# Hybrid decoder layer on one core: one 512-column product for the high and low parts of the tokens in the channel-major projections

## Chip, cores and metric

The kernel runs on one core of a Trainium2 chip. The metric is the device time of one execution in microseconds (us), as the median of several runs. TensorE multiplies matrices, VectorE (DVE) and ScalarE (ACT) do the elementwise work, GpSimd (POOL) a little of it, and SyncE (SP) issues the loads and stores.

## What is computed

One mixer layer on 256 tokens of width 2048, in float32. The input is normalised and modulated (h), a wide projection gives the inputs of two branches, gated DeltaNet (32 value heads of 128) and mLSTM (8 heads), and their merged output goes through one more projection and a norm. Cut to what matters here:

```python
h = rms_norm(x, norm_pre_w) * (1.0 + scale) + shift          # (256, 2048)
proj = h @ w_in                                              # all inputs of both branches
qkv = causal_conv_silu(gdn_qkv, gdn_conv_w)                  # 8192 channels
o_a = gated_delta_rule(q_a, k_a, v_a, g_log, beta)
y_a = (rms_norm(o_a, gdn_norm_w) * silu(gdn_z)) @ w_proj_gdn
qk = causal_conv_silu(ml_qk, mlstm_conv_w)                   # 2048 channels
h_b = mlstm_chunkwise(q_b, k_b, v_b, ml_i + b_i, ml_f + b_f)
y_b = (sigmoid(ml_o) * rms_norm(h_b) * silu(ml_z)) @ w_proj_mlstm
out = (sigmoid(gate_a) * y_a + sigmoid(gate_b) * y_b) @ w_out
x = x + gate * rms_norm(out, norm_post_w)

def causal_conv_silu(x, w):                                  # 4 taps along the tokens
    xp = pad(x, 3 rows in front)
    return silu(sum(xp[:, j:j + s] * w[j] for j in range(4)))
```

## The kernel before

**Two parts of each number.** Every projection is computed from float32 values split into a high part (rounded to fp32r by a copy on ScalarE, line 168) and a low part (value less high part, on VectorE or GpSimd, line 169). A product of two such numbers is three matmuls, `mm3` (lines 215 to 217): high x high, high x low, low x high, summed in PSUM. The tokens stand in `h_hi` and `h_lo`, two tiles of 16 chunks k of 128 rows by 256 tokens.

**The stream.** `Stream` (lines 62 to 113) runs through units of weights. A unit is one load of 1 MB (128 partitions by 2048 floats, issued by SP into one of three `raw` buffers) and two items of 1024 columns. For each item `prep_w` makes the high part `whi` and the low part `wlo` (four buffers each), some items ahead of TensorE; `use` then issues the matmuls; after that `Side.step` lets each side generator go on to its next `yield`. So one step of side work follows each item. The side generators hold the rest: convolution, attention, gates. `side.debt` (lines 37 to 55) is a rough count of VectorE time that the side work has asked for, with 2.1 us forgiven per step (`STEP_US`, line 26); only the triangular inverse (`base_inverse`) waits for it, through `side.room`.

**Stages.** A start part projects 14 groups while the modulation is still being computed. Then come eight periods of gated DeltaNet, `gdn_period`: a channel-major group of 512 channels (`add_proj_t`, pair 2zg), a token-major group for z (`add_proj_n`), and a second channel-major group (pair 2zg+1). Then four mLSTM pairs, each beginning with a channel-major group, the first also with the groups for o and z, the others with extra loads for the gate row. At the end are the two projections of the branches (`add_proj_y`) and the output projection. There are 20 channel-major groups in all.

**A channel-major group.** The weights are the stationary operand (128 channels) and the tokens the moving one (256 columns). Four units of four chunks k each; every item takes two chunks and all four channel blocks n, 24 matmuls. The four results share two PSUM banks of 512 columns (`pj` has four), and are complete only at the end of the group. `conv_silu` (lines 558 to 573) then scales them by the last tap on ScalarE (line 561), waits some steps, adds the other three taps on VectorE from PSUM (line 567), one channel block per step, and applies SiLU (line 570). `gdn_stage1` goes on with the products of q and k, the decay and the scaling; `base_inverse` inverts 32-row blocks on VectorE; `gdn_stage2` joins them with small matmuls and applies them one period later.

Of the kernel before, what the change touches and what calls it, by code (L numbers as in the profile page):

```python
# [7 lines left out]
F32 = mybir.dt.float32  # L8
# [7 lines left out]
P = 128  # L16
S = 256
# [99 lines left out]
def hybrid_layer_kernel(  # L117
# [41 lines left out]
    def load_w(src):  # L159
        raw = wp.tile([P, 2048], F32, name="raw", tag="raw", bufs=3)  # L160
        c = 0
        for s_ in src if isinstance(src, tuple) else (src,):
            SP.dma_start(raw[:, c:c + s_.shape[1]], s_)
            c += s_.shape[1]
        return raw
# [391 lines left out]

    def conv_silu(ps, taps, dst, hi=None, late=0):

        for n in range(4):  # L560
            A.activation(dst[:, n], ps[n // 2][:, (n % 2) * S:(n % 2 + 1) * S], AF.Copy, scale=taps(n, 3))
        yield from wait(1 + late)
        for n in range(4):
            src = ps[n // 2][:, (n % 2) * S:(n % 2 + 1) * S]
            side.debt += 1.45
            for sh in (1, 2, 3):
                V.scalar_tensor_tensor(dst[:, n, sh:], src[:, 0:S - sh], taps(n, 3 - sh), dst[:, n, sh:],  # L567
                                       op0=ALU.mult, op1=ALU.add)
            yield
        A.activation(dst, dst, AF.Silu)  # L570
        if hi is not None:
            A.copy(hi, dst[:, 0:2])
        yield

# [28 lines left out]

    def gdn_stage1(p, ps, res):

        z = p % 2
        qs = bp.tile([P, 4, S], F32, name="qs", tag="qs")
        qh = bp.tile([P, 2, S], F32R, name="qh", tag="qh", bufs=1)
        yield from conv_silu(ps, lambda n, j: late_c["gcv"][:, (p * 4 + n) * 4 + j:(p * 4 + n) * 4 + j + 1], qs, qh,
                             0 if z else 3)  # L610
        gb = decay_rows(2 * p)
# [25 lines left out]
        if z == 0:  # L637
            res["eq"] = bp.tile([P, 2, 2], F32, name="eq", tag="eq", bufs=3)
            res["rr"] = bp.tile([P, 2, 2, S], F32, name="rr", tag="rr")
        rk = bp.tile([P, 2], F32, name="rk", tag="rk")  # L640
# [84 lines left out]
    def gdn_stage2(zg, res, zr):  # L725
# [81 lines left out]
        for g, z, h, c in heads:  # L807
            T.matmul(po[z][:, h * P:(h + 1) * P], au[z][:, h, 0:128], ys[:, 0, c], start=True, stop=True)
            o2 = po[z][:, S + h * P:S + (h + 1) * P]
            T.matmul(o2, au[z][:, h, 128:256], ys[:, 0, c], start=True, stop=False)  # L810
            T.matmul(o2, au[z][:, h, 512:640], ys[:, 1, c], start=False, stop=True)  # L811
        so = bp.tile([P, 2, 2, 2], F32, name="so", tag="so")
        ons = []
# [39 lines left out]

    def period_tail(zg, ps, res, zr):
        yield from gdn_stage1(2 * zg + 1, ps, res)
        yield
        side.add(base_inverse(zg, res, zr), 2)

    zrs = [{} for _ in range(8)]

    def add_z(zg):
        def z_after(ps):
            sz = bp.tile([P, 2, 512], F32, name="sz", tag="sz", bufs=3)
            for b in range(2):
                A.activation(sz[:, b], ps[b], AF.Silu)
            zrs[zg]["sz"] = sz
        add_proj_n(16 + zg, z_after)

    def gdn_period(zg):
        res = {}  # L870
        add_proj_t(2 * zg, lambda ps: side.add(gdn_stage1(2 * zg, ps, res)))
        add_z(zg)
        add_proj_t(2 * zg + 1, lambda ps: side.add(period_tail(zg, ps, res, zrs[zg])))


    def mlstm_qk(m, ps, r):
        gb = decay_rows(32 + 2 * m)
        qk = bp.tile([P, 4, S], F32, name="mqk", tag="qs")
        yield from conv_silu(ps, lambda n, j: late_c["mcv"][:, (m * 4 + n) * 4 + j:(m * 4 + n) * 4 + j + 1], qk)
# [65 lines left out]
    def mlstm(m):  # L945
# [22 lines left out]
        def gate_after(ps, func):  # L968
            sg = bp.tile([P, 2, 512], F32, name="sg", tag="sz", bufs=3)
            for b in range(2):  # L970
# [13 lines left out]
        def gated():  # L984

            sg = bp.tile([P, 2, 512], F32, name="sg", tag="sz", bufs=3)
            SP.dma_start(sg, gate_dr[7 + m])
# [8 lines left out]
        gate_unit = add_gate_unit if m else None  # L996
        add_proj_t(24 + m, lambda ps: side.add(mlstm_qk(m, ps, r)), gate_unit)
        add_proj_n(28 + m, v_after, gate_unit)
# [55 lines left out]
    def add_proj_y(src_dr, w, nk2, mk, hf, after):  # L1054

        st_ = {}
        for k2 in range(nk2):
# [5 lines left out]
            def prep(h, raw, k2=k2):  # L1063
                if h == 0:
                    ahi = yp.tile([P, 2, S], F32R, name="yhi", tag="yhi", bufs=2)
                    alo = yp.tile([P, 2, S], F32R, name="ylo", tag="ylo", bufs=2)
                    split(st_[k2], ahi, alo)
                    st_["s", k2] = (ahi, alo)
                return prep_w(h, raw)
# [42 lines left out]
    def merge(hf, yb):  # L1112

        fp = late["fp"]
        if hf == 0:
            late["m"] = (hp.tile([P, KC, S], F32R, name="m_hi", tag="a_hi"),
                         hp.tile([P, KC, S], F32R, name="m_lo", tag="a_lo"))
        m_hi, m_lo = late["m"]
# [9 lines left out]
        for k2 in range(hf * 4, hf * 4 + 4):  # L1128
            ps = gtile("mtp")
            for kk in range(2):  # L1130
                for b in range(2):
                    T.transpose(ps[:, kk * S + b * P:kk * S + (b + 1) * P],
                                late["mg"][:, b, (2 * k2 + kk) * P:(2 * k2 + kk + 1) * P], ident)
            hi = m_hi[:, 2 * k2:2 * k2 + 2].rearrange("p a b -> p (a b)")
            A.copy(hi, ps)
            V.tensor_tensor(m_lo[:, 2 * k2:2 * k2 + 2].rearrange("p a b -> p (a b)"), ps, hi.bitcast(F32),
                            op=ALU.subtract)
            yield
# [176 lines left out]
```

## Time and profile before

| | |
|---|---|
| median of 3 runs | 1634.56 us (1633.07 to 1636.01) |
| profiled execution, its own time | 1634.3 us |
| its span, first to last instruction | 1632.5 us |
| TensorE busy | 1595.8 us, 98% |
| VectorE busy | 1137.3 us, 70% |
| ScalarE busy | 937.5 us, 57% |
| granted TensorE clock | 0.997 |
| read from HBM | 354.40 MB, 227 GB/s with the writes |

A group line of the profile gives line, engine, operation, output <- inputs, shapes and count, then busy time and mean time of one, then the idle time just before them. Matmuls overlap one another, so the mean time of one is longer than the time from one start to the next; the chain in order of time and the single instructions show the latter. A period means the stretch from one step of an attention pair to the same step of the next.

### The profile page before, as it was taken

What the parts mean: (1) busy time and instruction counts of PE and PEld (TensorE: products, weight loads), DVE (VectorE), ACT (ScalarE), POOL (GpSimd) and SP (SyncE); (2) the same over time, 40 slices, a digit from 0 to 9 for tenths busy, and PEclk for the clock granted to TensorE, in tenths of its full rate; (3) what the DMA queues carried; (4) which work ended last, traced back from release to release, by engine and by line L of the source; (5) the groups of instructions that cost most, each with busy time, mean ns of one, the idle gap of its engine ahead of it and who ended that gap; (6) DMA issues with size and microseconds to landing.
All of it is one profiled execution on the core that took longest, in us unless ns stands there. A gap on an engine that the chain in (4) does not pass through costs nothing.

```text
span 1632.5 us, 25436 instructions
## 1 busy us (share of the span) xinstructions
PE 1595.8 (98%) x9844; PEld 1398.7 (86%) x9844; DVE 1137.3 (70%) x1793; ACT 937.5 (57%) x1496; POOL 241.7 (15%) x191
## 2 busy tenths in 40 slices
PE   6999999999999999999999999999999999999997
PEld 4888887799998999999898989889988788888886
DVE  5585556665678787969686969685878556756654
ACT  7744446665655575666666666665565544444443
POOL 3877760000000010000000000000100000100101
PEclk9999999999999999999999999999999999999999
DMA  9998775765454555454546464646888668766572
GB/s 370 387 364 321 280 272 180 259 245 187 166 197 165 183 175 185 165 184 160 185 161 197 162 198 152 193 167 247 299 301 310 236 235 301 275 233 252 194 278 103
DMA packets 96259, 372.37 MB, mean 228 GB/s; under 512 B 26261, under 2 KB 46213, under 8 KB 58249
## 3 DMA queue, kind: packets, MB, share of 16 engines
q1 hardware_dynamic: 96138, 370.75, 63.9%
q8 instruction: 77, 1.26, 0.3%
q14 instruction: 44, 0.36, 0.1%
HBM read 354.40 MB, written 16.31 MB: 227 GB/s over the span
## 4 chain that ended last, share of the span: by engine, by line
PE 78%; issue 13%; DVE 3%; ACT 2%; DMA 2%; POOL 1%; SPq 0%; DVEq 0%; POOLq 0%; ACTq 0%
PE pn L217 34%; PE pt L217 27%; PE py L217 8%; DVE wlo L169 1%; ACT whi L168 1%; POOL mg L1123 1%; PE psa L217 1%; DMA raw<-in_dram 1%; PE mq L766 1%; PE mz L774 1%; PE mp L741 1%; PE pt L848 0%; DMA ar<-in_dram 0%; PE po L811 0%; PE pc L801 0%
## 5 line engine op out<-in xcount | busy, mean ns | idle before, releaser
L169 DVE TENSOR_TENSOR wlo<-raw,whi 128x1024 fp32r<-128x1024 f32 x450 | 552.7, 1237 | 273.3 <-ACT whi L168 272.4
L168 ACT CAST whi<-raw 128x1024 fp32r<-128x1024 f32 x514 | 532.0, 1051 | 313.2 <-PE pn L217 145.7
L217 PE MATMUL pt<-h_hi,whi 128*128 128x256 f32 x1280 | 368.1, 288 | 0.0
L217 PE MATMUL pt<-h_hi,wlo 128*128 128x256 f32 x1280 | 362.6, 283 | 1.9 <-DVE wlo L169 1.9
L217 PE MATMUL pt<-h_lo,whi 128*128 128x256 f32 x1280 | 362.0, 283 | 0.0
L217 PE MATMUL pn<-whi,h_hi 128*128 128x512 f32 x896 | 354.3, 395 | 3.5 <-ACT whi L168 3.4
L217 PE MATMUL pn<-wlo,h_hi 128*128 128x512 f32 x896 | 350.5, 391 | 3.0 <-DVE wlo L169 3.0
L217 PE MATMUL pn<-whi,h_lo 128*128 128x512 f32 x896 | 350.4, 391 | 0.0
L217 PEld LDWEIGHTS pt<-h_hi,wlo 128*128 128x128 f32 x1280 | 245.1, 191 | 2.8 <-DVE wlo L169 2.7
L217 PEld LDWEIGHTS pt<-h_hi,whi 128*128 128x128 f32 x1280 | 245.2, 192 | 1.3
L217 PEld LDWEIGHTS pt<-h_lo,whi 128*128 128x128 f32 x1280 | 245.3, 192 | 0.2
L217 PEld LDWEIGHTS pn<-whi,h_hi 128*128 128x128 f32 x896 | 169.1, 189 | 40.1 <-ACT whi L168 3.8
L217 PEld LDWEIGHTS pn<-wlo,h_hi 128*128 128x128 f32 x896 | 169.2, 189 | 38.4 <-DVE wlo L169 4.3
L217 PEld LDWEIGHTS pn<-whi,h_lo 128*128 128x128 f32 x896 | 169.0, 189 | 35.8 <-POOL h_lo L169 0.3
L169 POOL TENSOR_TENSOR wlo<-raw,whi 128x1024 fp32r<-128x1024 f32 x64 | 153.6, 2408 | 44.2 <-ACT whi L168 44.2
L217 PE MATMUL py<-whi,yhi 128*128 128x512 f32 x384 | 150.6, 392 | 0.3 <-ACT vt L953 0.3
L217 PE MATMUL py<-whi,ylo 128*128 128x512 f32 x384 | 149.5, 389 | 0.0
L217 PE MATMUL py<-wlo,yhi 128*128 128x512 f32 x384 | 149.4, 389 | 0.0
L405 DVE TENSOR_TENSOR part<-pn,part 128x512 f32<-128x512 f32 x112 | 74.0, 687 | 48.0 <-PE pn L217 48.0
L168 ACT CAST yhi<-ya 128x512 fp32r<-128x512 f32 x48 | 29.9, 622 | 124.7 <-PE py L217 122.9
L169 DVE TENSOR_TENSOR ylo<-ya,yhi 128x512 fp32r<-128x512 f32 x48 | 33.2, 692 | 90.4 <-ACT yhi L168 88.4
L567 DVE SCALAR_TENSOR_TENSOR qs<-pt,gcv,qs 128x255 f32<-128x255 f32 (+2 forms) x192 | 92.2, 480 | 4.6
(243 smaller groups left out, 1800.5 us busy)
## 6 DMA issues: line engine op xcount, KB each, us to landing
raw<-in_dram SPq DMA_DIRECT2D x259, 1024.0 KB
ar<-in_dram SPq DMA_DIRECT2D x32, 1024.0 KB
raw<-in_dram SPq DMA_DIRECT2D x28, 512.0 KB
ya<-o_dr SPq DMA_DIRECT2D x32, 256.0 KB
gate_dr<-part SPq DMA_DIRECT2D x11, 512.0 KB
gb<-rows SPq DMA_DIRECT2D x20, 256.0 KB
ug<-ud SPq DMA_DIRECT2D x32, 128.0 KB
o_dr<-oT SPq DMA_DIRECT2D x16, 256.0 KB
```

The costliest lines, as they stand in the source:

```text
L168: A.copy(hi, src)
L169: (eng or V).tensor_tensor(lo, src, hi.bitcast(F32), op=ALU.subtract)
L217: T.matmul(ps, l, r, start=start and i == 0, stop=stop and i == 2, skip_group_check=True)
L405: V.tensor_tensor(part[g][:, b], st_["ps"][b], part[g][:, b], op=ALU.add)
L567: V.scalar_tensor_tensor(dst[:, n, sh:], src[:, 0:S - sh], taps(n, 3 - sh), dst[:, n, sh:], op0=ALU.mult, op1=ALU.add)
L741: T.matmul(pss[t][o:o + 32, m * 32:(m + 1) * 32], um(m)[r:r + 32, o:o + 32], yc[r:r + 32, m], start=True, stop=True)
L766: T.matmul(psp[64:128, m * 64:(m + 1) * 64], um(m)[0:64, 64:128], y0[:, m], start=True, stop=True)
L774: T.matmul(psz[0:64, m * 64:(m + 1) * 64], p2[64:128, m], x0[64:128, m, 64:128], start=True, stop=True)
L1123: G.tensor_tensor(mcols(b, hf, cg), mcols(b, hf, cg), s_, op=ALU.add)
```

## The change

The high and low parts of the tokens now lie next to each other for each k, in one tile `h2` (16 chunks x 2 parts x 256). A channel-major group is computed in two halves of two channel blocks each. For each k and block there is one matmul of 512 columns, high weights times both parts of the tokens, and one of 256, low weights times the high tokens, added to the second half of the bank. So the bank holds high x high in its first 256 columns and the two small products in the others. They are summed on the way out: ScalarE copies the second half to `qs`, VectorE adds the first to it into `xc`, ScalarE scales by the last tap, and VectorE adds the other taps from `xc`.

Each load now takes eight chunks k of 256 columns, so it comes in pieces of 1 KB. The first half of a group is convolved while the second half is being projected. The wait that was set by hand for even pairs goes, the first mLSTM pair waits until seven periods have been applied in place of a fixed number of steps, and some buffers move: `rr` alternates between a ring shared with the split y inputs and one buffer of its own, z gates have four buffers in place of three.

```diff
+            n = s_.shape[1] * (s_.shape[2] if len(s_.shape) > 2 else 1)
+            d = raw[:, c:c + n]
+            SP.dma_start(d.rearrange("p (k c) -> p k c", k=s_.shape[1]) if len(s_.shape) > 2 else d, s_)
...
-    h_hi = hp.tile([P, KC, S], F32R, name="h_hi", tag="a_hi")
-    h_lo = hp.tile([P, KC, S], F32R, name="h_lo", tag="a_lo")
+    h2 = hp.tile([P, KC, 2, S], F32R, name="h2", tag="a")
+    h_hi, h_lo = h2[:, :, 0], h2[:, :, 1]
...
     def add_proj_t(g, after, extra=None):
         for t in range(4):
             def use(h, hi, lo, t=t):
-                if t == 0 and h == 0:
+                if t % 2 == 0 and h == 0:
                     st_["ps"] = [jtile(f"pt{i}") for i in range(2)]
-                for kc in range(2):
-                    k = t * 4 + h * 2 + kc
-                    for n in range(4):
-                        o = kc * 512 + n * P
-                        mm3(st_["ps"][n // 2][:, (n % 2) * S:(n % 2 + 1) * S], hi[:, o:o + P], lo[:, o:o + P],
-                            h_hi[:, k], h_lo[:, k], k == 0 and n % 2 == 0, k == KC - 1 and n % 2 == 1)
-            stream.add(w_in[g][:, t * 2048:(t + 1) * 2048], prep_w, use, after=
-                       (lambda: after(st_["ps"])) if t == 3 else None)
+                for kc in range(4):
+                    k = t % 2 * 8 + h * 4 + kc
+                    for n in range(2):
+                        ps, o = st_["ps"][n], kc * 256 + n * P
+                        if k < KC - 1:
+                            T.matmul(ps, hi[:, o:o + P], h2[:, k].rearrange("p a t -> p (a t)"), start=k == 0,
+                                     stop=False, skip_group_check=True)
+                        T.matmul(ps[:, S:2 * S], lo[:, o:o + P], h_hi[:, k], start=False, stop=False,
+                                 skip_group_check=True)
+                        if k == KC - 1:
+                            T.matmul(ps, hi[:, o:o + P], h2[:, k].rearrange("p a t -> p (a t)"), start=False,
+                                     stop=True, skip_group_check=True)
+            src = w_in[g].rearrange("p (k c) -> p k c", c=512)[:, t % 2 * 8:t % 2 * 8 + 8, t // 2 * 256:t // 2 * 256 + 256]
+            stream.add(src, prep_w, use, after=
+                       (lambda t=t: after(t // 2, st_["ps"])) if t % 2 else None)
...
-    def conv_silu(ps, taps, dst, hi=None, late=0):
...
+    def conv_half(half, ps, taps, dst):
+        d = dst[:, 2 * half:2 * half + 2]
+        for n in range(2):
+            A.copy(d[:, n], ps[n][:, S:2 * S])
+        yield
+        xc = yp.tile([P, 2, S], F32, name="xc", tag="ya", bufs=3)
+        side.debt += 0.8
+        for n in range(2):
+            V.tensor_tensor(xc[:, n], ps[n][:, 0:S], d[:, n], op=ALU.add)
+        for n in range(2):
+            A.activation(d[:, n], xc[:, n], AF.Copy, scale=taps(2 * half + n, 3))
+        for n in range(2):
+            yield
+            side.debt += 1.45
+            for sh in (1, 2, 3):
+                V.scalar_tensor_tensor(d[:, n, sh:], xc[:, n, 0:S - sh], taps(2 * half + n, 3 - sh), d[:, n, sh:],
+                                       op0=ALU.mult, op1=ALU.add)
+    def add_conv(g, taps, then, extra=None, rank=1):
+        qs = {}
+        def after(half, ps):
+            if half == 0:
+                qs["t"] = bp.tile([P, 4, S], F32, name="qs", tag="qs")
+            def chain():
+                yield from conv_half(half, ps, taps, qs["t"])
+                if half:
+                    yield
+                    yield from then(qs["t"])
+            side.add(chain(), rank)
+        add_proj_t(g, after, extra)
...
-    def gdn_stage1(p, ps, res):
-        yield from conv_silu(ps, lambda n, j: late_c["gcv"][...], qs, qh, 0 if z else 3)
+    def gdn_stage1(p, qs, res):
+        A.activation(qs, qs, AF.Silu)
+        A.copy(qh, qs[:, 0:2])
+        yield
...
+            pool, tag, bufs = (bp, "rr", 1) if p // 2 % 3 == 2 else (yp, "y4", 2)
+            res["rr"] = pool.tile([P, 2, 2, S], F32, name="rr", tag=tag, bufs=bufs)
...
+        applied[0] += 1                      # in gdn_stage2, behind the products po
...
-        yield from wait(8 if m == 0 else 1)
+        yield
+        while applied[0] < 7:
+            yield
...
-                    ahi = yp.tile([P, 2, S], F32R, name="yhi", tag="yhi", bufs=2)
-                    alo = yp.tile([P, 2, S], F32R, name="ylo", tag="ylo", bufs=2)
+                    y2 = yp.tile([P, 2, 2, S], F32R, name="y2", tag="y4", bufs=2)
```

The tiles `m_hi` and `m_lo` of the output projection become views of one tile in the same way.

More of the change, by code (lines that the diff above doesn't have):

```diff
@@ L852, in gdn_stage2, with period_tail @@
             SP.dma_start(o_dr[4 * zg + 2 * z:4 * zg + 2 * z + 2].rearrange("h d t -> d h t"), oT)
[L854 to L855 removed]
+    def period_tail(zg, qs, res, zr):
+        yield from gdn_stage1(2 * zg + 1, qs, res)
         yield
@@ L870, in gdn_period, with mlstm_qk @@
         res = {}
[L871 removed]
+        add_conv(2 * zg, gdn_taps(2 * zg), lambda qs: gdn_stage1(2 * zg, qs, res))
         add_z(zg)
[L873 to L876 removed]
+        add_conv(2 * zg + 1, gdn_taps(2 * zg + 1), lambda qs: period_tail(zg, qs, res, zrs[zg]))
+    def mlstm_qk(m, qk, r):
         gb = decay_rows(32 + 2 * m)
[L878 to L879 removed]
+        A.activation(qk, qk, AF.Silu)
+        yield
         av = [tt[:, b, 64 + 2 * m:66 + 2 * m] for b in range(2)]
@@ L996, in mlstm @@
         gate_unit = add_gate_unit if m else None
-        add_proj_t(24 + m, lambda ps: side.add(mlstm_qk(m, ps, r)), gate_unit)
+        add_conv(24 + m, lambda n, j: late_c["mcv"][:, (m * 4 + n) * 4 + j:(m * 4 + n) * 4 + j + 1],
+                 lambda qk: mlstm_qk(m, qk, r), gate_unit)
         add_proj_n(28 + m, v_after, gate_unit)
```

44 lines of the change are left out of this document (16 added, 28 removed).

## Prediction

> **What bounds the kernel now.** I read the page first, for shares and the chain; then the chain in order of time; then the matmuls one by one where two widths meet; then the busy time of a period, the longest waits, and the distance between the vector engine's output and its use. The page:
>
> ```profile
> span 1632.5 us, 25436 instructions
> PE 1595.8 (98%) x9844; PEld 1398.7 (86%) x9844; DVE 1137.3 (70%) x1793; ACT 937.5 (57%) x1496; POOL 241.7 (15%) x191
> PE pn L217 34%; PE pt L217 27%; PE py L217 8%; DVE wlo L169 1%; ACT whi L168 1%; POOL mg L1123 1%; PE psa L217 1%; DMA raw<-in_dram 1%; PE mq L766 1%; PE mz L774 1%; PE mp L741 1%; PE pt L848 0%; DMA ar<-in_dram 0%; PE po L811 0%; PE pc L801 0%
> L217 PE MATMUL pt<-h_hi,wlo 128*128 128x256 f32 x1280 | 362.6, 283 | 1.9 <-DVE wlo L169 1.9
> raw<-in_dram SPq DMA_DIRECT2D x259, 1024.0 KB
> ```
>
> TensorE is busy in 98% of the span and the products named pt, the ones that the change touches (3 x 1280), are 27% of the chain. Their 283 ns is a pipelined duration, not what one costs. That is read from the chain in order of time:
>
> ```profile
> 348.67 23.03 PE pt L217 x192
> 371.70 21.79 PE pn L217 x96
> 512.62 2.91 PE pt L217 x22
> 791.16 1.02 PE mp L741 x32
> 875.01 1.02 PE mp L741 x32
> ```
>
> 192 products of 256 columns take 23.03 us: 0.120 us each. 96 products of 512 columns take 21.79 us: 0.227 each. The last two rows are the same step of two neighbouring periods (two channel-major groups and one z group): a period is 83.85 us. Its TensorE work by these prices is 384 x 0.120 + 96 x 0.227 = 67.9 us, and the rest is the small products of the attention part between the pieces. In such a period the engines do this:
>
> ```profile
> core 0: us, PE busy (x) PEld busy (x) DVE busy (x) ACT busy (x) POOL busy (x), PEclk, DMA share, GB/s
> 791.16:875.01 83.85, 83.07 (x674) 77.82 (x675) 66.56 (x139) 53.80 (x100) 5.16 (x9) 1.00 0.53 175
> 480.00:520.00 40.00, 36.80 (x290) 35.30 (x290) 36.84 (x69) 20.18 (x28) 1.43 (x3) 1.00 0.42 142
> 1102.00:1250.00 148.00, 147.16 (x1056) 135.34 (x1055) 109.97 (x143) 81.50 (x154) 9.57 (x12) 1.00 0.79 284
> ```
>
> TensorE has 0.8 us of gap in the period, at clock 1.00: it is the bound. VectorE is the runner-up with 66.56 of 83.85. In the second stretch the order is reversed: TensorE is idle for 3.2 of 40 us while VectorE is busy for 36.84. The waits, over the whole span:
>
> ```profile
> DVE wlo L169 <- ACT whi L168: 272.4, 195, 6.2
> ACT whi L168 <- PE pt L217: 76.2, 53, 3.1
> ACT whi L168 <- DMA raw<-in_dram: 21.2, 14, 4.1
> ACT qs L570 <- DVE qs L567: 15.3, 7, 5.5
> PE pn L217 <- DVE wlo L169: 3.0, 3, 1.7
> PE pt L217 <- DVE wlo L169: 1.9, 4, 1.1
> ```
>
> The preparation waits for TensorE to give buffers back (76.2 us), and TensorE waits for the low parts in seven places, 4.9 us in all. How far ahead the preparation is at its tightest in a settled period, VectorE first and then the TensorE product that uses that piece:
>
> ```profile
> 842.39 1.23 DVE L169 TENSOR_TENSOR wlo<-raw,whi 128x1024 fp32r<-128x1024 f32 x1
> ...
> 846.79 0.28 PE L217 MATMUL pt<-h_hi,wlo 128*128 128x256 f32 x1
> ```
>
> The piece is ready at 843.62 and used at 846.79: a lead of 3.2 us, about one item (24 products, 2.88 us). Which piece belongs to which product is counted off in order, one low part for each item.
>
> **The change, part by part.**
>
> *TensorE.* For each block of channels and each k, three products of 256 columns (0.360 us) become one of 512 and one of 256. That order, alternating, is not in the trace, but its two joints are:
>
> ```profile
> 348.28 0.39 PE L217 MATMUL pn<-whi,h_lo 128*128 128x512 f32 x1
> 348.50 0.28 PE L217 MATMUL pt<-h_hi,whi 128*128 128x256 f32 x1
> 348.62 0.28 PE L217 MATMUL pt<-h_lo,whi 128*128 128x256 f32 x1
> ```
>
> ```profile
> 371.42 0.28 PE L217 MATMUL pt<-h_hi,wlo 128*128 128x256 f32 x1
> 371.54 0.40 PE L217 MATMUL pn<-whi,h_hi 128*128 128x512 f32 x1
> 371.77 0.40 PE L217 MATMUL pn<-wlo,h_hi 128*128 128x512 f32 x1
> 372.00 0.39 PE L217 MATMUL pn<-whi,h_lo 128*128 128x512 f32 x1
> ```
>
> A 256 right behind a 512 holds the engine for about 0.12 us (348.50 to 348.62), a 512 right behind a 256 for 0.23 (371.54 to 371.77). Steady prices give the pair 0.227 + 0.120 = 0.347, and the joints much the same. So each triple saves 0.013 us: 1280 x 0.013 = **16.6 us**, all of it where TensorE is on the chain. Bounds: if every 256 took only 0.113, half the price of a 512, the pair is 0.340 and the gain 25.6 us; if the 512 costs 0.236 (as 371.77 to 372.00, rounded up) and the 256 0.120, the pair is 0.356 and the gain 5 us. I take 0.347, since the long runs give both intervals and the joints add up to it. And it is paid nearly in full: 27% of the span is 441 us, and 3840 products at 0.120 are 461, so all but 20 us of them lie on the chain.
>
> The Trainium skill ("TensorE: Matmul & The Clock Gate", section "Back-to-back issue gap") speaks against this: it puts the warm gap at columns over 2.4 GHz plus about 2.5 ns, so dropping one product saves only that, an estimate of 1280 x 2.5 ns = 3.2 us. The trace does not agree: by that rule 256 columns take 109 ns and 512 take 216, and the rows give 120 and 227, some 13 ns above the columns' own time at either width. Its consequence is weighed among the rivals.
>
> *VectorE and ScalarE.* Each half group adds two copies out of PSUM on ScalarE and two sums on VectorE. The nearest rows, same 256 columns:
>
> ```profile
> L914 ACT COPY hn<-pnum x16: 345/364/413, 1080.7 to 1283.2; 128x256 f32<-128x256 f32 x16
> L966 DVE TENSOR_TENSOR hn<-hn,sg x4: 419/420/425, 1101.6 to 1102.6; 128x256 f32<-128x256 f32 x4
> L963 DVE SCALAR_TENSOR_TENSOR hn<-hn,mso,sg x16: 472/480/485, 1091.5 to 1290.8; 128x256 f32<-128x256 f32 x16
> L567 DVE SCALAR_TENSOR_TENSOR qs<-pt,gcv,qs x192: 474/481/489, 382.2 to 1008.9; 128x255 f32<-128x255 f32 x64, 128x254 f32<-128x254 f32 x64, 128x253 f32<-128x253 f32 x64
> ```
>
> ScalarE: 80 copies x 0.364 = 29 us; in a period 2.9, so 57 of 82 us: hidden. VectorE: 80 sums x 0.42 = 34 us; in a period 8 x 0.42 = 3.4, so 70 of a new period of 82.2 (83.85 less 128 x 0.013): hidden by some 12 us of gaps, as long as these fall where they are needed. The shifted multiply-adds now read SBUF instead of PSUM: 0.480 against 0.481, nothing. The scaled copies and the SiLU only move.
>
> Where VectorE is already the bound the sums are in the open. That is around 483 to 516 us, the only period with the triangular inverse on VectorE but no second-stage products on TensorE. The planner allows 2.1 us of side work per item (line 26) and the low part takes 1.23, so 3.33 against an item of 2.88: 0.45 behind per item. The new item is 8 x 0.347 = 2.78, 0.55 behind: ten items make 1.1 us more, plus 0.8 for the half of a group's four sums that falls there (the first half is now done while that group still runs, ahead of the crowd). About 0.7 more in the mLSTM part, where VectorE also sums the gate row. I charge **2.6 us**. From below, the 3.2 us of idle TensorE in that stretch vanish because the convolution is spread; from above, all 34 us of sums in the open.
>
> *New waits.* In each half ScalarE's scaled copy waits for VectorE's sum, queued behind low parts. Behind it on ScalarE stand the high parts, for which the low parts and then TensorE wait. Today's like is the SiLU behind the multiply-adds: 15.3 us in 7 waits, 5.5 the longest. The cover is the lead of 3.2 us or more; without it each us would be paid. I charge nothing beyond the 2.6.
>
> *PSUM.* A half takes two of the four projection banks and frees them after copy and sum, one or two items on; the next half begins in the other two. Nothing.
>
> *Loads.* 80 loads of 1 MB come in pieces of 1 KB instead of 8 KB, on the same queue in the same order. If the pieces doubled the transfer time, the eight loads of a period (8.4 of its 14.7 MB) would lift the share from 0.53 to 0.83: covered. In the mLSTM part three groups (12.6 of 42 MB) would lift 0.79 to 1.03. Taken at no cost, the nearest row being the settled period.
>
> *The rest.* Dropping the hand-set waits of the even pairs starts their attention part some items sooner; it waits for what it needs anyway. The first mLSTM pair now waits for the seventh period's last products. Moving rr and the y halves into a shared ring and a fourth z buffer adds no instruction. Nothing for these.
>
> **Sum.** The profiled execution took 1634.3 us (span 1632.5 and 1.8 around it), 0.3 under the median of the runs. 1634.3 - 16.6 + 2.6 = **1620 us**.
>
> **The rivals.**
>
> *A: the pair is dear.* If a product of 512 next to one of 256 holds the array 0.236, the gain is 5 us, less the 2.6: 1632. For it: the rows behind 371.54. Against: the joint at 348.50 and the 0.120 and 0.227 of long runs. By the Trainium skill's rule of the same section, 3.2 less 2.6 lands on 1634, the same case.
>
> *B: VectorE's order becomes the bound.* VectorE's low parts wait for ScalarE within the period:
>
> ```profile
> L169 DVE TENSOR_TENSOR wlo<-raw,whi 128x1024 fp32r<-128x1024 f32 x25 | 30.5, 1220 | 13.8 <-ACT whi L168 13.8
> ```
>
> If these 13.8 us can't shrink, VectorE's path is 66.6 + 13.8 = 80.4 now, 83.8 with the sums, and no shorter than today's period: no gain, about 1632. If each of the four hand-overs of a period also costs it 0.4 us, the period is 85.4: 1.6 x 8 periods + 2 for mLSTM, so 15 over, 1649, **slower**. It decides where the lead of 3.2 us is used up. Against it: most of that wait is ScalarE waiting for TensorE's buffers, and it shrinks once TensorE is quicker.
>
> *C: the spread pays.* With half of each convolution moved into its own group, the 3.2 us of idle TensorE go and nothing is added: 1634.3 - 16.6 - 3.2 = 1614.5, down to 1610 with the other bound of the pair in part. For it: in the crowded stretch the chain runs through the multiply-adds between low parts:
>
> ```profile
> 509.67 0.49 DVE qs L567
> 510.19 0.48 DVE qs L567
> 510.67 0.49 DVE xx L703
> 511.34 1.23 DVE wlo L169
> ```
>
> Against: the sums come on top, and the inverse fills what is left free.
>
> *D: the 1 KB pieces show* in the mLSTM part, at twice the time: 0.03 x 148 us plus as much of delay, 8 us: 1628. For it: share 0.79. Against: only 21.2 us of waits for raw in all, none of TensorE's.
>
> **How the numbers follow.** Forecast (1616 to 1626) 0.60; C 0.14; D 0.06; A 0.06; B without loss 0.05; B with loss 0.09. About 0.2%, 3.3 us, is what a measurement of this kernel can tell from none. Faster: 0.60 + 0.14 + 0.06 = 0.80; same: A and the even B, 0.11; slower 0.09. The forecast, C and D hold 0.80 and lie between 1610 and 1630.
>
> **What would show it.** Right: pt rows x1280 with 512 and x1280 with 256 columns; a half group's chain piece of 64 products in 11.1 us; periods near 82 us with VectorE near 70; TensorE's waits for the low part near 7 us. Wrong on the price: long runs of pairs at 0.355 or 0.340. Wrong on cover: dozens of waits of pt for wlo, and ScalarE's scaled copies waiting for the sums by 30 us or more. Wrong on loads: waits of whi for raw well above 21 us between 1100 and 1260.

## The result, and the profile after

The changed kernel takes 1718.45 us, median of 5 runs (1714.40 to 1719.18), against 1635.27 us before (5 runs, 1633.07 to 1636.88): ratio 1.0499, 95% interval 1.0485 to 1.0514. It is 83 us slower; some 14 us faster had been forecast. The profiled execution took 1718.45 us.

First the chain by engine of the kernel before, then the page of the changed kernel (busy time of the engines, the chain by engine, the group of the low parts, two groups of matmuls):

```profile
PE 78%; issue 13%; DVE 3%; ACT 2%; DMA 2%; POOL 1%; SPq 0%; DVEq 0%; POOLq 0%; ACTq 0%
```

```profile
span 1716.4 us, 23051 instructions
PE 1620.6 (94%) x8564; PEld 1345.1 (78%) x8564; DVE 1166.0 (68%) x1873; ACT 958.6 (56%) x1576; POOL 250.7 (15%) x191
PE 47%; DVE 16%; issue 15%; ACT 10%; DMA 8%; POOL 2%; SPq 2%; DVEq 0%; ACTq 0%; POOLq 0%
L171 DVE TENSOR_TENSOR wlo<-raw,whi 128x1024 fp32r<-128x1024 f32 x450 | 552.1, 1238 | 320.4 <-ACT whi L170 319.8
L537 PE MATMUL pt<-h,whi 128*128 128x512 f32 x1200 | 441.6, 408 | 1.8 <-ACT whi L170 1.7
L539 PE MATMUL pt<-h,wlo 128*128 128x256 f32 x1280 | 358.2, 285 | 7.3 <-DVE wlo L171 7.3
```

1280 products are gone (9844 to 8564), and yet TensorE is busy longer than before, 1620.6 us against 1595.8, and idle longer too: span less busy time is 95.8 us, before it was 36.7. So of the 84 us by which the span grew, 59 are idle time of TensorE and 25 are busy time. The chain shows that TensorE is no longer the bound throughout: it carried 78% and now carries 47%, while VectorE, ScalarE and the DMAs went from 7% to 34% together. The pt rows themselves wait for little. What the new pair of products costs is seen where nothing else interferes, in the first groups (TensorE by time; the first product of three half groups in a row):

```profile
396.27 0.39 PE L537 MATMUL pt<-h,whi 128*128 128x512 f32 x1
...
407.57 0.39 PE L537 MATMUL pt<-h,whi 128*128 128x512 f32 x1
...
418.87 0.39 PE L537 MATMUL pt<-h,whi 128*128 128x512 f32 x1
```

32 pairs take 11.30 us, 0.353 each. A group of 64 triples took 23.03, now it takes 22.60: 0.43 x 20 groups = 8.6 us won on TensorE. So some 92 us were lost. To see where, take the step mp, the small matmuls that follow each triangular inverse and read its result ycmp (the matmul row of the tile mp, before and then after; the columns are the shortest, median and longest duration in ns, then the first and last start):

```profile
L741 PE MATMUL mp<-ycmp,au x256: 191/191/212, 535.0 to 1105.9; 32*32 32x32 f32 x128
```

```profile
L774 PE MATMUL mp<-ycmp,au x256: 184/191/257, 543.8 to 1183.0; 32*32 32x32 f32 x128
```

From the first to the last, 570.9 us have become 639.2: 68 us are lost between the first and the last of the eight inverses. Ahead of them the kernel loses 9 us, behind them 7. The waits of the changed kernel (who waits for whom: total, times, longest):

```profile
DVE wlo L171 <- ACT whi L170: 319.8, 221, 8.4
...
ACT qs L579 <- DVE xc L577: 108.3, 32, 8.5
...
ACT whi L170 <- DMA raw<-in_dram: 50.5, 19, 10.1
...
ACT whi L170 <- PE pt L537: 22.5, 17, 2.8
...
PE mp L774 <- DVE ycmp L748: 18.5, 5, 8.3
...
PE pn L219 <- DVE wlo L171: 13.5, 14, 4.9
```

The second row is new: ScalarE's scaled copy waits for VectorE's sum, 3.4 us a time. The fourth was 76.2 us before: in the channel-major groups the preparation rarely waits for TensorE any more, so it is rarely ahead. What one such wait does, in the changed kernel, VectorE, ScalarE and TensorE by time:

```profile
490.29 1.22 DVE L171 TENSOR_TENSOR wlo<-raw,whi 128x1024 fp32r<-128x1024 f32 x1
491.43 0.75 DVE L577 TENSOR_TENSOR xc<-pt,qs 128x256 f32<-128x256 f32 x2
...
491.94 0.91 ACT L579 ACTIVATE qs<-xc,gcv 128x256 f32<-128x256 f32 x2 [7.07 <-DVE xc L577]
...
492.76 2.93 ACT L170 CAST whi<-raw 128x1024 fp32r<-128x1024 f32 x3
...
493.82 1.23 DVE L171 TENSOR_TENSOR wlo<-raw,whi 128x1024 fp32r<-128x1024 f32 x1 [0.57 <-ACT whi L170]
...
495.11 0.38 PE L539 MATMUL pt<-h,wlo 128*128 128x256 f32 x1 [0.45 <-DVE wlo L171]
```

The sums stand on VectorE behind steps of the inverse and low parts, and are done at 492.2. ScalarE had stood still for 7.07 us with the next high parts behind the scaled copy. Then the low part waits for the high part, and TensorE for the low part: ready at 495.05, used at 495.11. Of the lead of 3.2 us nothing is left here.

Such a pause cost more than its own length here. The granted clock around the longest wait for ycmp (8.3 us; three stretches of the changed kernel, columns as in the prediction, so that the clock is the third number from the end):

```profile
640.00:659.00 19.00, 12.94 (x69) 10.28 (x67) 4.77 (x12) 11.07 (x23) 1.63 (x4) 1.00 0.49 114
659.00:669.20 10.20, 6.70 (x47) 5.89 (x48) 9.04 (x29) 3.37 (x6) 0.00 (x0) 0.51 0.68 218
669.20:680.00 10.80, 10.80 (x119) 9.08 (x118) 9.82 (x21) 5.40 (x10) 0.00 (x0) 0.99 0.37 115
```

```profile
666.44 0.43 PE pt L537
666.87 0.21 PE pt L539
...
671.59 0.23 PE pt L537
671.82 0.12 PE pt L539
```

The wait lasts from 654.2 to 662.5 us. The clock falls to half within it, near 659.2, and stays there until about 669.1, so that for 6.6 us after the wait TensorE needs 0.64 us for a pair instead of 0.35 (the second fence is the chain in order of time). Over the execution the mean granted clock is 0.979, before it was 0.997: a shortfall of 36 us against 5, part of it within the pauses themselves. That is how TensorE can be busy longer with fewer products: the 8.6 us won and the 25 us of added busy time make 33 us. That the clock is all of these 33 us is not shown.

### The profile page after: what moved, and what is told of

Same layout as the page of the kernel before. It is cut to its first block, busy times and chain, and to the rows that moved or that the text cites. A ratio compares the mean times of both kernels' runs of the same rounds, so it can differ in the third digit from the quotient of the medians.

```text
span 1716.4 us, 23051 instructions
## 1 busy us (share of the span) xinstructions
PE 1620.6 (94%) x8564; PEld 1345.1 (78%) x8564; DVE 1166.0 (68%) x1873; ACT 958.6 (56%) x1576; POOL 250.7 (15%) x191
## 4 chain that ended last, share of the span: by engine, by line
PE 47%; DVE 16%; issue 15%; ACT 10%; DMA 8%; POOL 2%; SPq 2%; DVEq 0%; ACTq 0%; POOLq 0%
PE pn L219 23%; PE pt L537 8%; PE py L219 7%; DVE wlo L171 6%; PE pt L539 4%; ACT whi L170 4%; DMA gb<-rows 3%; DVE qs L584 3%; DVE au L690 1%; DMA ug<-ud 1%; DVE gacc L1060 1%; DMA ar<-in_dram 1%; POOL mg L1160 1%; POOL dd L620 1%; ACT qs L639 1%
## 5 line engine op out<-in xcount | busy, mean ns | idle before, releaser
L171 DVE TENSOR_TENSOR wlo<-raw,whi 128x1024 fp32r<-128x1024 f32 x450 | 552.1, 1238 | 320.4 <-ACT whi L170 319.8
L219 PE MATMUL pn<-whi,h 128*128 128x512 f32 x1792 | 573.4, 397 | 4.9 <-ACT whi L170 4.9
L537 PE MATMUL pt<-h,whi 128*128 128x512 f32 x1200 | 441.6, 408 | 1.8 <-ACT whi L170 1.7
L219 PEld LDWEIGHTS pn<-whi,h 128*128 128x128 f32 x1792 | 341.9, 191 | 79.3 <-ACT whi L170 6.9
L219 PE MATMUL pn<-wlo,h 128*128 128x512 f32 x896 | 355.5, 397 | 13.5 <-DVE wlo L171 13.5
L539 PE MATMUL pt<-h,wlo 128*128 128x256 f32 x1280 | 358.2, 285 | 7.3 <-DVE wlo L171 7.3
L537 PEld LDWEIGHTS pt<-h,whi 128*128 128x128 f32 x1200 | 230.3, 192 | 54.4 <-ACT whi L170 2.8
L539 PEld LDWEIGHTS pt<-h,wlo 128*128 128x128 f32 x1280 | 246.4, 192 | 16.3 <-DVE wlo L171 13.5
L219 PE MATMUL py<-whi,y 128*128 128x512 f32 x768 | 240.3, 392 | 2.2 <-ACT vt L990 2.2
L219 PEld LDWEIGHTS pn<-wlo,h 128*128 128x128 f32 x896 | 171.1, 191 | 54.7 <-DVE wlo L171 20.1
L219 PE MATMUL py<-wlo,y 128*128 128x512 f32 x384 | 149.9, 390 | 0.0
```

The source lines that it names most:

```text
L171: (eng or V).tensor_tensor(lo, src, hi.bitcast(F32), op=ALU.subtract)
L219: T.matmul(ps, l, r, start=start and i == 0, stop=stop and i == 2, skip_group_check=True)
L537: T.matmul(ps, hi[:, o:o + P], h2[:, k].rearrange("p a t -> p (a t)"), start=k == 0, stop=False, skip_group_check=True)
L539: T.matmul(ps[:, S:2 * S], lo[:, o:o + P], h_hi[:, k], start=False, stop=False, skip_group_check=True)
```

## The experiments

Each time stands beside runs of the kernel before on the same chip (1634.0 to 1635.5 us). e1 to e9 ran once, the others four or five times. Two explanations run through them: ScalarE's hand-over (theory H: the scaled copy waits for the sum and holds up the high parts) and VectorE's time (theory T, or V: 34 us more work on an engine without slack). Their rivals are the loads of 1 KB pieces and the planner's order, that is, the places at which `side.debt` lets the inverse go on.

**One suspect at a time, on the changed kernel.** The length of an inverse is counted here in low parts that stand on VectorE between its first tile, nsu, and its last, ycmp. In the kernel before it was 20 (18 the first, 13 the last); with the 0.8 us of planner's debt per half the eight last 18, 25, 21, 19, 26, 25, 26 and 14, and four times the next one begins before the last has ended. An inverse has two bounces, in which a tile goes out to DRAM and comes back in another layout. On SP the bounces of two inverses then stand together (the SP queue of the changed kernel, x is the number of issues):

```profile
629.09 7.09 SPq L165 DMA_DIRECT2D raw<-in_dram  x2
636.27 0.53 SPq L613 DMA_DIRECT2D gb<-rows  x1
636.86 0.43 SPq L741 DMA_DIRECT2D xd<-xx  x1
642.98 2.77 SPq L744 DMA_DIRECT2D xcmp<-xd  x4
645.79 3.77 SPq L710 DMA_DIRECT2D ud<-au  x8
649.67 2.75 SPq L714 DMA_DIRECT2D ug<-ud  x4
652.47 25.98 SPq L165 DMA_DIRECT2D raw<-in_dram  x5
```

No weight load is issued for some 16 us. The chain through the longest wait for ycmp passes here: ug lands at 657.4 us, VectorE goes on with the next inverse's nsu at 659.5, ycmp comes behind it, and TensorE goes on at 662.5. Four edits:

```diff
e1_no_debt
-        side.debt += 0.8
e2_scale_dve
-            A.activation(d[:, n], xc[:, n], AF.Copy, scale=taps(2 * half + n, 3))
+            V.tensor_scalar(d[:, n], xc[:, n], taps(2 * half + n, 3), None, op0=ALU.mult)
e3_long_loads        # the host lays a half group's weights out in one piece
-            src = w_in[g].rearrange("p (k c) -> p k c", c=512)[...]
+            src = w_in[g][:, t * 2048:(t + 1) * 2048]
e5_split_bounce      # two items between out and back; later waits two shorter
+        yield from wait(2)
```

> The changed kernel without the 0.8 that each half's two sums add to the planner's count of VectorE time; no instruction is added or removed. In the program the triangular inverse then ends 1 to 7 items ahead of the next period's inverse, where in the changed kernel it ends 1 or 2 items behind it in four of seven periods. Theory P (the late inverse puts its two bounces through DRAM into one place of SP's queue, and no weights are loaded for 16 to 22 us; four places, about 11 us of idle TensorE each): 1675 us or less, and no gap over 13 us between weight loads after 600 us. Theory H (ScalarE waits for VectorE's sums and holds up the high parts): unchanged, 1710 to 1722. Theory L (1 KB loads): unchanged.

> The changed kernel with the copy scaled by the last tap on VectorE in place of ScalarE, so ScalarE no longer waits for VectorE's sum; VectorE has 80 more instructions of some 0.25 us (20 us in all). Theory H: the 108 us of ScalarE's waits for xc go and with them up to 56 us of idle TensorE: 1665 to 1685. Theory P: the four long gaps between weight loads stay, 1700 to 1722. Theory L: 1715 to 1725.

> The changed kernel with the channel-major weights laid out by the host so that each load is contiguous again, 8 KB for a partition; the order of all instructions stays. Theory L: waits of the high part for raw fall from 50.5 us to about 21 and the time to 1650 or less. Theories P and H: 1705 to 1718.

> The changed kernel with two items of other work between the two halves of each bounce through DRAM (out and back in), so that weight loads are issued between them and SP does not stand at a landing; the inverse's place in the plan is unchanged. Theory P, if SP's queue is what costs: the gaps of 16 to 22 us between weight loads fall under 13, time 1670 to 1690. If the late inverse costs in another way, or theory H: 1705 to 1720.

Measured: 1698.3, 1692.3, 1707.2 and 1707.1 us, that is 20, 26, 11 and 11 less than the change. None is the cause by itself, and e1 and e2 lie outside the range of every theory named for them. Without the debt the inverses last 17, 20, 24, 17, 20, 24, 17 and 13 low parts and never overlap, but the waits for xc stay, 116.4 us; with the scaled copy on VectorE these are gone, but VectorE has the work. In e5 other issues stand on SP between two weight loads for 11.1 us at most (16 to 21 at four places in the change, both counted from 380 to 1240 us), and yet it gains only 11: the queue was a part of the loss at most.

**Together, and relief by GpSimd.** e7 has all four edits; e8 is the change, e9 is e7, each with a fifth of the low parts on GpSimd (`share[1] = 0.2` instead of 0.0); e13 is e7 with `STEP_US = 2.4` instead of 2.1, which makes every inverse last 18 low parts.

> The changed kernel with the four edits tried singly put together: no 0.8 in the planner's count, scaled copy on VectorE, contiguous loads, bounces in two steps. If the four losses lie in different places their gains add up (20 + 26 + 11 + 11 us): 1650. If they are the same idle time of TensorE seen in four ways: 1675 to 1690. If the lead is regained everywhere: 1620.

> The changed kernel with a fifth of the low parts made on GpSimd behind the start part too, which takes 5 x 1.23 = 6 us a period off VectorE and changes no place in the plan. Theory V (VectorE is behind its plan because of the added sums): 1650 to 1685. If only the hand-over or SP's queue counts: 1705 to 1718.

> The four edits together and a fifth of the low parts on GpSimd. Theory V on top of the rest: 1615 to 1635. If VectorE's load doesn't matter once the order is mended: as the four alone.

> The changed kernel with the four edits that were run together (no extra debt, scaled copy on VectorE, 8 KB loads, two steps between the way out and the way back of each DRAM bounce: 1682.9 us) and 2.4 us instead of 2.1 us taken off the planner's debt per step, so that each inverse lasts 18 low parts. Theory Q (uneven plan): about 1665, waits of the step mp for ycmp (12.4 us) gone. Theory T (VectorE has no time left where the inverse runs): 1680 to 1695, with the waits moved to other side products (au, on) or grown.

Measured: 1682.9; 1724.6; 1703.4; 1686.8 (ratio 1.0307, 1.0274 to 1.0339). The four gains, 69 us added up, give 36, as would be expected if they emptied in part the same idle time. GpSimd makes it worse both times, against the theory that relief of VectorE pays: a low part takes it 2462 ns, VectorE 1238, and TensorE now waits 20.8 us for GpSimd's low parts in e8 and 17.2 in e9. An even plan brings nothing: in e13 all inverses but the first and last do last 18 low parts.

**The halves without the sums.** e6 computes three 256-column products in one accumulator again, and the convolution reads it directly; halves, 1 KB loads and moved buffers stay. e10 adds the 8 KB loads, e11 also `STEP_US = 2.4`. e12 is e6 with the sums as bare VectorE work:

```diff
e6_halves_only
-                        T.matmul(ps, hi[...], h2[:, k]..., ...)            # and the one for lo
+                        mm3(ps[:, 0:S], hi[:, o:o + P], lo[:, o:o + P], h_hi[:, k], h_lo[:, k], k == 0, k == KC - 1)
-            A.copy(d[:, n], ps[n][:, S:2 * S])                             # and debt, sum, scaled copy of xc
+            A.activation(d[:, n], ps[n][:, 0:S], AF.Copy, scale=taps(2 * half + n, 3))
e12_halves_sum
+            V.tensor_tensor(xc[:, n], ps[n][:, 0:S], d[:, n], op=ALU.add)   # nobody reads xc
             for sh in (1, 2, 3):
```

> The changed kernel with the three 256-column products back, summed in one place of PSUM: halves, 1 KB loads, early convolution and all moved buffers stay; the copies out of PSUM, the sums and the hand-over from VectorE to ScalarE are gone, and TensorE has its 16.6 us back to do. The plan of the inverse is that of the kernel without the 0.8, 1698 us. If the sums and the hand-over are what costs there: 1640 to 1655. If the halves and the earlier convolution cost by themselves: 1690 or more.

> The kernel with the halves alone (three 256-column products in one accumulator, no copy, no sum: 1662.1 us, 28 above the kernel before), and the first weights of each pair laid out so that a load takes 8 KB in one piece per partition. Theory P (the loads' 1 KB pieces make the weights late in the halves, and this is most of the 28 us): about 1642, and TensorE's long pauses fall from 49 us to near the 31 of the kernel before. Theory Q (the loads are hidden; the planner's uneven spread of the triangular inverse, 17, 20, 24 low parts instead of 20 each, makes TensorE wait for ycmp and for banks): 1655 to 1662.

> As the run with halves and 8 KB loads, and the planner takes 2.4 us instead of 2.1 us off its debt per step, so that every inverse lasts 18 low parts in the order of VectorE's instructions (17, 20, 24 otherwise; 20 each in the kernel before). Theory Q (the uneven plan is most of the 28 us): about 1637 to 1645, waits of the step mp for ycmp gone. Theory P (the loads): no more than 3 us below the run without it. Theory R (a shorter inverse asks more of VectorE than it can give, whatever the spread): slower than the run without it, by up to 10 us, with longer waits for ycmp.

> The kernel with the halves alone (1662.1 us) and, in each half, the two VectorE sums of 0.375 us beside the convolution, reading the accumulator and written where nobody reads them: VectorE's 30 us of work come back, the pair of products, the copy, the hand-over to ScalarE's scaled copy and the planner's debt do not. Theory T (VectorE's time itself is what the sums cost, since VectorE is behind the planner's order in the middle of the kernel): 1680 to 1692, most of the 53 us that the sums cost beside the 16.6 us that they win on TensorE. Theory H (the hand-over: ScalarE's copy stands in front of the weights' high parts until the sum is done): 1662 to 1668.

Measured: 1662.1; 1659.4 (ratio 1.0147, 1.0127 to 1.0168); 1660.4 (1.0153, 1.0122 to 1.0185); 1680.0 (1.0272, 1.0249 to 1.0295). e6 lies between the ranges of its two theories. The 8 KB loads gain about 3 us here, little more than the runs differ among themselves. The even plan gains nothing, but e11 doesn't price it alone: mp's waits for ycmp fall from 5.0 us in e10 to 1.1, and pt's waits for accumulators rise from 7.8 to 17.8. The halves cost 28 us in this form, but a part of that is e6's own (a group row of e6, idle time behind the last bar):

```profile
L219 PE MATMUL pt<-h,whi 128*128 128x256 f32 x2560 | 475.6, 287 | 10.0 <-DVE qs L571 8.7 <-ACT whi L170 1.2
```

TensorE waits 8.7 us for accumulators that VectorE still reads; the changed kernel, which frees them at the sum, has no such wait. So e6 doesn't say what the halves cost in the change. The idle sums cost 18 us, the least that theory T gave and far more than theory H did. They also read the accumulators, though, and the same wait grows from 8.7 to 15.4 us, so up to 7 of the 18 us can be banks held longer.

**Time or hand-over.** e14 is e1 with one `yield` more, so that the scaled copy is issued an item after the sum:

```diff
             V.tensor_tensor(xc[:, n], ps[n][:, 0:S], d[:, n], op=ALU.add)
+        yield
         for n in range(2):
             A.activation(d[:, n], xc[:, n], AF.Copy, scale=taps(2 * half + n, 3))
```

e16 is the kernel before with the idle sums of e12. e15 forms the sums on GpSimd, from two copies by ScalarE, without the debt and with the scaled copy an item later; e17 is e15 with the edits of e3 and e5.

```diff
+            A.copy(xc[:, n], ps[n][:, 0:S])
-            V.tensor_tensor(xc[:, n], ps[n][:, 0:S], d[:, n], op=ALU.add)
+            G.tensor_tensor(xc[:, n], xc[:, n], d[:, n], op=ALU.add)
```

> The changed kernel without the extra planner's debt (1698.3 us), and ScalarE's scaled copies issued one item later than the sums, so that a low and a high part of the next weights stand between them. Theory H (ScalarE is held up behind the sums: its waits for xc sum to 116 us there): about 1675 to 1682, waits of the scaled copy for xc under 30 us. Theory T (VectorE's time is what counts, ScalarE's wait is only the time by which VectorE is behind): 1693 to 1703, and the waits for xc go over to the next place where ScalarE needs VectorE (Silu of the group, decay mask).

> The changed kernel with the sums taken off VectorE: ScalarE copies both halves of the product out of the accumulator (80 more copies of about 0.364 us, 29 us), GpSimd adds them (80 times about 0.75 us, by its 128x256 subtraction in the kernel before), and the scaled copy comes an item later; no extra debt. Theory T (VectorE's 34 us): 1650 to 1665, VectorE busy some 30 us less. Theory H (the hand-over): also below the changed kernel, but not below the run with the later hand-over by more than 5 us. If ScalarE's order is the bound, 1690 or more, with the high parts late and VectorE's waits for them longer than 304 us.

> The kernel before (whole groups, three products) and, beside each of its convolution's channel blocks, one VectorE sum of 0.375 us which nobody reads: VectorE's 30 us of work alone, in the order of the kernel before. Theory T (VectorE is at its limit in the middle of the kernel whatever the order): 1650 to 1660, the same 18 to 20 us as beside the halves. Theory S (the kernel before has slack for it, and it is the halves' shorter distances that make VectorE's time count): 1634 to 1640.

> The run with the sums on GpSimd, with 8 KB loads and two steps between the way out and the way back of each DRAM bounce: the version in which each suspected cost is taken off. If VectorE's time, the hand-over and the loads are all that the change costs beside the halves, TensorE's 16.6 us come through and it ends at 1640 to 1650; by theory T alone (loads hidden) no different from the run without these two.

Measured: e14 1653.3 (ratio 1.0108, 1.0093 to 1.0124); e15 1657.5 (1.0132, 1.0115 to 1.0149); e16 1655.9 (1.0128, 1.0110 to 1.0146); e17 1646.2 (1.0066, 1.0042 to 1.0090). The one `yield` is worth 45 us, about twice the most that theory H had expected of it. The waits of e1 and then of e14:

```profile
DVE wlo L171 <- ACT whi L170: 304.4, 208, 9.3
...
ACT qs L578 <- DVE xc L576: 116.4, 35, 8.7
```

```profile
DVE wlo L171 <- ACT whi L170: 268.7, 203, 10.2
...
ACT qs L579 <- DVE xc L576: 30.7, 15, 5.1
...
PE mp L774 <- DVE ycmp L748: 7.7, 7, 2.2
```

ScalarE waits 86 us less for the sums, VectorE 36 us less for the high parts, and the mean granted clock is back at 0.992 from 0.979. TensorE's idle time falls by 24 us and its busy time by 21. The plan is not the reason: the inverses last the same number of low parts in e1 and e14. But the `yield` also puts the multiply-adds an item later, and no run moves the scaled copy alone. e7 warns against giving the hand-over all of the 45 us: it has no such wait, no debt, long loads and split bounces, and is 30 us slower than e14, with 19 us more work on VectorE.

e16 shows VectorE's own price in the order of the kernel before, with no plan moved, no hand-over and no matmul that waits for these reads of the accumulators: 33.4 us of sums (its two rows below) cost 20.5 us.

```profile
L567 DVE TENSOR_TENSOR xc<-pt,qs 128x256 f32<-128x256 f32 x64 | 26.7, 418 | 0.0
L567 DVE TENSOR_TENSOR xc<-pt,mqk 128x256 f32<-128x256 f32 x16 | 6.7, 417 | 0.0
```

e15 lies in the range that theory T gave it, but is no faster than e14 with the sums on VectorE, so it doesn't show T: the sums leave VectorE, and 31.8 us more of copies on ScalarE and GpSimd's contention with VectorE come (last section). e17 ends in the range for every cost taken off; the 8 KB loads and split bounces gain 11 us over e15.

**The next hand-over.** In e17 the longest wait of ScalarE for VectorE is the Silu's for the convolution, 45.3 us. e18 is e17 with the Silu one item later, e19 the same with the sums on VectorE (e14, e3 and e5).

```diff
                 if half:
-                    yield
+                    yield from wait(2)
```

> The run with sums on GpSimd, 8 KB loads and split bounces (1646.2 us), and each group's Silu one item later behind its convolution. Theory H (every place where ScalarE waits for VectorE in front of the weights' high parts is paid, as at the scaled copy): ScalarE's wait of the Silu for qs falls from 45 us to under 20, and the time to 1625 to 1637. Theory N (that wait lies where TensorE has its lead, and the rest is the halves' order itself): 1643 to 1650.

> The same kernel with the sums on VectorE, as in the change, ScalarE copying the low halves alone: the run with the later scaled copy (1653.3 us), 8 KB loads, split bounces and the later Silu. Theory T (VectorE's time counts at 18 to 20 us for the sums): 10 to 20 us above the run with GpSimd. Theory H alone (it is the order, not the engine): within 5 us of it; in both cases below 1653.

Measured: 1666.9 (1.0201, 1.0187 to 1.0215) and 1664.0 (1.0175, 1.0161 to 1.0188): 21 and 18 us slower than e17. Both theories had e18 no slower than 1650 and e19 below 1653. That the two lie 3 us apart is what theory H said: in this order too, taking the sums from VectorE to GpSimd gains nothing. The waits of e17 and then of e18:

```profile
ACT L640 <- DVE qs L585: 45.3, 12, 7.9
...
ACT dd L629 <- POOL dd L621: 15.1, 9, 5.2
...
PE pn L219 <- DVE wlo L171: 2.9, 3, 1.7
```

```profile
ACT dd L629 <- POOL dd L621: 44.8, 14, 6.8
...
ACT L640 <- DVE qs L585: 29.4, 10, 4.9
...
PE pn L219 <- DVE wlo L171: 10.3, 16, 1.7
```

16 us of one wait go and 30 us of the next come, the decay mask's. TensorE now waits 16 times for low parts in the z groups, where it waited three times. The edit also moves the plan: the later inverses last 18, 21, 18, 21 low parts where e17 has 17, 20, 24, 17. So a hand-over an item later is no remedy as such. It seems to depend on the place that it lands on, which no run shows by itself, and I have no rule for that. No version tried beats the kernel before; the nearest, e17, is 0.66% slower.

## Why the prediction was wrong, point by point

*The step that failed: "New waits ... I charge nothing beyond the 2.6."* The wait was named, and what stands behind it. The price was taken from the lead of 3.2 us. But a wait lasts 3.4 us in the mean and up to 8.5, since the sum stands on VectorE behind steps of the inverse and low parts (as at 491 us). The lead is seldom there any more: the preparation's waits for pt fell from 76.2 to 22.5 us. From e1 to e14 the step measures 45 us, the multiply-adds' later place included. The rival B had the mechanism and its condition, "where the lead of 3.2 us is used up", but took 0.4 us per hand-over from nothing in the trace; 45 us over 40 hand-overs are 1.1 each. Its chance of 0.09 rested on that price. Of the prediction's own signs of being wrong on cover, one is plainly there: the scaled copies wait 108.3 us for the sums, where 30 was named. The waits of pt for wlo are 16, not dozens.

*"Hidden by some 12 us of gaps".* The size of a sum was right (0.417 against 0.42 us), the cover was not: 20.5 us of the 33.4 show in the order of the kernel before (e16), 11 to 18 beside the halves (e12). The gaps of VectorE in that period were 17.3 us, 13.8 of them waits for high parts, each tied to a place between two low parts. So gaps that are an engine's own waits were no cover here for work put ahead of them.

*The planner's debt of 0.8 us* was seen in the diff and priced nowhere. It makes an inverse last up to nine low parts longer (26 against 17 in e1), and moves the bounces on SP with it: 20 us (e1). Following the planner's count to the order on VectorE and SP would have found it.

*TensorE* was right in direction: 8.6 us instead of 16.6, within its bounds of 5 and 25.6. The pair takes 0.353 us, not 0.347, and so lies nearer to rival A's 0.356. The Trainium skill ("TensorE: Matmul & The Clock Gate", section "Back-to-back issue gap") gives its rule for a matmul taken by itself, which the prediction left out; the estimate of 3.2 us from it was off by 5.4 us, my 16.6 by 8.0.

*Loads* charged at nothing: in the change the 8 KB pieces are worth 11 us, beside the halves 3 (one run of e6 against four of e10). Waits for raw rose from 21.2 to 50.5 us, by 21 up to the last inverse and by 9 in the mLSTM part, where rival D put them.

*PSUM at nothing* held for the change: no row shows a pt waiting for xc. *The spread* of the convolution (rival C) brought nothing that a run shows.

*Not thought of:* the clock halved in the longest pause and stayed so for 6.6 us behind it.

As a chain of differences: 8.6 us won; 20 lost for the debt, 45 for the hand-over with what moved beside it, and 27 that are left: e14 is 18.0 above the kernel before, in spite of the 8.6. VectorE's 20.5 are most of these, if they count there as in e16; e15 and e18, which gain nothing by taking the sums off VectorE, don't confirm it, since they add work elsewhere. Some 6 us, for the halves, the copies and the 1 KB loads together, stay open, and so does how far the parts add up at all: the four single edits did not.

## What to carry to other kernels

When an engine that prepares operands is made to wait for a busy one, price the wait by how far that engine is behind its order at that place, not by the mean gap and not by a lead that one wait can use up; put other work of the waiting engine between the two. Before that, add the new work alone, with nobody waiting for it: such a run (e16) and one with the hand-over moved (e14) go far to split time from order in two kernels. And when a planner's count is changed with the work, follow what it moves on every queue.

## What the runs showed of the hardware

Around the end of a pause of TensorE of 8.3 us the granted clock was 0.51 over 10.2 us, and products took nearly twice as long (0.64 us a pair, 0.35 later). The Trainium skill ("TensorE: Matmul & The Clock Gate", section "Part 1: The HAM clock gate") has half clock after an idle window of about 3.4 us and full clock after a busy one; the trace agrees: the clock fell some 5 us after the pause began, more than one such window, and was full again 6.6 us after work resumed.

GpSimd and VectorE slowed each other in e15. GpSimd's sums took 871 ns in the mean, but 742 in the median and up to 1799; its subtraction of the same 128x256 shape took 747 in the kernel before. VectorE's products of two SBUF operands beside them (groups of e14, then of e15):

```profile
L584 DVE SCALAR_TENSOR_TENSOR qs<-xc,gcv,qs 128x255 f32<-128x255 f32 x64 | 30.9, 483 | 0.0
...
L732 DVE TENSOR_TENSOR tmp<-xx,ug 128x28 f32<-128x28 f32 x8 | 1.7, 208 | 0.2
```

```profile
L585 DVE SCALAR_TENSOR_TENSOR qs<-xc,gcv,qs 128x255 f32<-128x255 f32 x64 | 33.1, 516 | 0.0
...
L733 DVE TENSOR_TENSOR tmp<-xx,ug 128x28 f32<-128x28 f32 x8 | 4.0, 502 | 0.2
```

The Trainium skill ("SBUF — State Buffer", section "SBUF: two separate sides") says that the two share a pair of ports which one of them holds for a whole instruction; the trace agrees. Of the eight small products of 128x28, four took 0.72 to 0.77 us, each beside a GpSimd sum, one 0.37, and three 0.21 as all eight did in e14. Most of the other widths of this product show no difference.
